# A hybrid decoder block on one core: 80 instead of 256 pair sums in retrieval, all gate masks on VectorE, and the row products behind the last mask

## The chip, the cores and the metric

One core of a Trainium2 chip runs the whole block in one launch. The metric is device time in microseconds (us). The kernel before took 3866.27 us (median of 3 runs, 3858.65 to 3869.51). The engines are TensorE (PE, with its weight loads PEld), VectorE (DVE), ScalarE (ACT), GpSimd (POOL) and SyncE (SP, which only issues transfers here). Each engine works through its own instructions strictly in the order in which they stand.

## The reference

The block is a mixer (windowed attention beside a state space model), a retrieval of single-neuron experts ("PEER"), and a final norm. The change lies in the retrieval, for 512 tokens, 8 heads, 128 keys for each half, the best 16 of each:

```python
def peer(h, w_query, sub_keys, expert_down, expert_up):
    q = (hf @ w_query).reshape(t, PEER_HEADS, 2, PEER_HALF)
    sc = jnp.einsum('thcd,hckd->thck', q, sub_keys)
    s_top, i_top = lax.top_k(sc, PEER_TOPK)                       # 16 of 128, twice
    cand = s_top[:, :, 0, :, None] + s_top[:, :, 1, None, :]      # 16 x 16 sums
    cand_idx = i_top[:, :, 0, :, None] * PEER_NKEYS + i_top[:, :, 1, None, :]
    best, sel = lax.top_k(cand.reshape(t, PEER_HEADS, 256), PEER_TOPK)
    idx = jnp.take_along_axis(cand_idx.reshape(t, PEER_HEADS, 256), sel, axis=-1)
    gates = jax.nn.softmax(best, axis=-1)
    # per token: a = x . expert_down[idx]; w = gelu(a) * gates; out = w @ expert_up[idx]
```

Both lists of 16 are sorted, so the sum of places (a, c) can be among the best 16 only if (a + 1)(c + 1) is at most 16.

## The kernel before

Everything is float32 from outside; the large products are made in three passes of a high and a low part (`whi`, `wlo`: ScalarE casts each weight tile, line 185; VectorE or GpSimd subtracts, line 187). Four stages matter here.

**Retrieval** (lines 907 to 957). For each head TensorE makes queries and scores; VectorE then takes the best 16 of 128 for each half and each of four blocks of 128 tokens (`top16`, lines 847 to 852: maximum of eight, its places, replace, again), adds all 16 x 16 pairs (`cand`, line 932), takes the best 16 of 256, and turns a place into the two indices by shift and mask (lines 944 to 951). An index is looked up by comparison with a ramp (`oh`, line 953, VectorE), a product on GpSimd (line 955) and a sum on VectorE (line 956). GpSimd also makes `wlo` of the query weights.

**Gates** (lines 1065 to 1102). Expert number i1 x 128 + i2; the last 160 of the 512 tokens are not treated densely. For the other 352 a dense gate table g_d is built. Sixteen tokens at a time (22 times, each in two halves, so 44) VectorE makes four masks of 128 x 1024 float16: `o1`, `o2` (lines 1088, 1089), and `g0`, `g1` (lines 1091, 1090); three of four `g1` are made on GpSimd (`ptt`). TensorE multiplies them (line 1098, 16 products for eight tokens), ScalarE copies to `stg` (line 1100), and a transfer stores it in DRAM.

**Row products** (`gathered`, lines 1029 to 1054). For the 160 other tokens 320 steps run beside everything else: each fetches one row of 1 MB by an indirect transfer that GpSimd issues (line 1010) and works it off in one long VectorE instruction (line 1016 for 160 "down" rows, lines 1025 and 1027 for 160 "up" rows). The buffers are two (h3_hi, h3_lo) until the second group of the main loop ends, then three. A step of `gathered` is taken by `paced`: 1.0 a block of 16 tokens in the gates, 1.25 at each of 16 places of a main loop group.

**Main loop** (lines 1155 to 1197). 16 groups: eight *forms* (line 1110: 48 matmuls of 352 columns, lines 201 to 203, then gelu) and 16 *up* products of 24 matmuls (lines 1185 to 1187), so 768 matmuls a group. The forms' results are multiplied by the gate table (line 1165), which a transfer `gt` reads back from g_d (line 1157). The first 21 forms are written ahead of the loop (line 1128) and need no gates.

The order on each engine is made when the program is built, by a scheduler that plays the program through with its own durations; it puts those 21 forms between retrieval and gate work as it sees fit.

Of the kernel before, what the change touches and what calls it, by code (L numbers as in the profile page):

```python
# [1 line left out]

# [4 lines left out]
F32 = mybir.dt.float32  # L7
# [3 lines left out]
U32 = mybir.dt.uint32  # L11
AF = mybir.ActivationFunctionType
OP = mybir.AluOpType
# [5 lines left out]
TT = 4  # L19
# [9 lines left out]
TB = 16  # L29
HB = 8  # L30
# [6 lines left out]
A_BUFS = 5  # L37
LEAD = 2
Z_EARLY = 4
GATHER_PACE = 1.25  # L40
GATE_PACE = 1.0
GATE_SCALE = 32768.0
NEG = -3.0e38
MAGIC = 12582912.0
# [15 lines left out]
def hybrid_block(tc, I, out, dbg=None):  # L60
    nc = tc.nc
# [32 lines left out]
    tt, ts, stt = nc.vector.tensor_tensor, nc.vector.tensor_scalar, nc.vector.scalar_tensor_tensor  # L94
# [235 lines left out]
    ptt = nc.gpsimd.tensor_tensor  # L330
# [130 lines left out]
    for i in range(8):  # L461
        p = head[i]
# [301 lines left out]
    for m in range(KT):  # L764
        p = mm_tile()
# [9 lines left out]
    for m in range(8):  # L775
        p = mm_tile()
# [15 lines left out]
    for m in range(KT):  # L792
        p = mm_tile()
# [32 lines left out]
    for m in range(KT):  # L826
        p = mm_tile()
# [16 lines left out]
    tk = pool("tk", "right", bufs=2)  # L844
    keys = tk.tile([128, 16, 128], F32, name="keys", bufs=1)
    nc.sync.dma_start(keys, I["sub_keys"])
    def top16(vals, idx, x, scratch):
        nc.vector.max(out=vals[:, 0:8], in_=x)
        nc.vector.max_index(out=idx[:, 0:8], in_max=vals[:, 0:8], in_values=x)
        nc.vector.match_replace(out=scratch, in_to_replace=vals[:, 0:8], in_values=x, imm_value=NEG)  # L850
        nc.vector.max(out=vals[:, 8:16], in_=scratch)
        nc.vector.max_index(out=idx[:, 8:16], in_max=vals[:, 8:16], in_values=scratch)
# [64 lines left out]
    for hd in range(8):  # L917
        stop = tk.tile([128, TT, 2, 16], F32, name="stop")
        itop = tk.tile([128, TT, 2, 16], U32, name="itop")
        if hd < 2:  # L920
            query_scores(opening[hd], hd, stop, itop, rstd)
        else:
            o = [mm_tile(), mm_tile(), aux_tile()]
            for qt in range(4):
                query_quarter(o, hd, qt, NB)
            query_scores(o, hd, stop, itop)
        best = tk.tile([128, TT, 16], F32, name="best")
        sel = tk.tile([128, TT, 16], U32, name="sel")
        for b in range(TT):
            cand = tk.tile([128, 256], F32, name="cand")  # L930
            cand2 = tk.tile([128, 256], F32, name="cand2")
            tt(cand.rearrange("p (a c) -> p a c", a=16), stop[:, b, 0, :, None].to_broadcast([128, 16, 16]),  # L932
               stop[:, b, 1, None, :].to_broadcast([128, 16, 16]), op=OP.add)
            top16(best[:, b], sel[:, b], cand, cand2)
        e = tk.tile([128, TT, 16], F32, name="ge")
        s8 = tk.tile([128, 2, TT], F32, name="s8")
        tt(e, best, best[:, :, 0:1].to_broadcast([128, TT, 16]), op=OP.subtract)
        act(e, e, AF.Exp)
        nc.vector.tensor_reduce(s8[:, 0], e, axis=AX.X, op=OP.add)
        nc.vector.reciprocal(s8[:, 1], s8[:, 0])  # L940
        tt(pk[:, :, 2, hd], e, s8[:, 1, :, None].to_broadcast([128, TT, 16]), op=OP.mult)
        itf = tk.tile([128, TT, 2, 16], F32, name="itf")
        nc.vector.tensor_copy(itf, itop)
        for c in range(2):
            ai = tk.tile([128, TT, 16], U32, name="ai")
            if c == 0:
                ts(ai, sel, 4, None, op0=OP.logical_shift_right)
            else:
                ts(ai, sel, 15, None, op0=OP.bitwise_and)
            af = tk.tile([128, TT, 16], F32, name="af")  # L950
            nc.vector.tensor_copy(af, ai)
            oh = tk.tile([128, TT, 16, 16], F32, name="oh")
            tt(oh.rearrange("p a b c -> p (a b) c"), iota[:, None, 0:16].to_broadcast([128, TT * 16, 16]),
               af.rearrange("p a b -> p (a b)")[:, :, None].to_broadcast([128, TT * 16, 16]), op=OP.is_equal)
            nc.gpsimd.tensor_tensor(oh, oh, itf[:, :, c, None, :].to_broadcast([128, TT, 16, 16]), op=OP.mult)
            nc.vector.tensor_reduce(pk[:, :, c, hd], oh, axis=AX.X, op=OP.add)
    close(tk)
# [56 lines left out]
    def gather_down(index, f, g, n):  # L1014
        r = rows_of("down_rows", index[:, n:n + 1])
        stt(r, r, 1.0, hrow, op0=OP.mult, op1=OP.mult, accum_out=f[:, n:n + 1])  # L1016
        if n % 16 == 15:
            w = f[:, n - 15:n + 1]
            act(w, w, AF.Gelu_apprx_tanh)
            tt(w, w, g[:, n - 15:n + 1], op=OP.mult)  # L1020
# [8 lines left out]
    def gathered():  # L1029
        downs = [(pick, fit, gate, n) for n in range(128)] + [(pick_x, fit_x, gate_x, n) for n in range(NX)]  # L1030
        ups = [("own", pick, fit, n) for n in range(128)] + [("x", pick_x, fit_x, n) for n in range(NX)]
        y = None
        for i in range(len(downs) + UP_LAG):
            if i < len(downs):
                if i == 128:
                    wide = slice(ND, NB)
                    token_rows(hrow, *(lambda ks, z=z: z[:, ks, None, wide].bitcast(F32).to_broadcast([128, 4, XQ, NX])
                                       for z in (h2_hi, h2_lo)), (("p k (i t) -> p k i t",), {"i": XQ}))
                gather_down(*downs[i])
                yield  # L1040
            if i >= UP_LAG:
                which, index, f, n = ups[i - UP_LAG]
                if n == 0:
                    y = state["gp"].tile([128, KT, 128], F32, name="yrow")
                gather_up(y, index, f, n)
                if which == "own" and n == 127:
                    gather_finish(y)
                if which == "x" and n == NX - 1:
                    for m in range(KT):
                        p = aux_tile()[:, 0:NX]  # L1050
                        nc.tensor.matmul(p, y[:, m], fold, start=True, stop=True)
                        xm = state["x1"][:, m, ND:NB]
                        stt(xm, p, mod[:, 80 + m:81 + m], xm, op0=OP.mult, op1=OP.add)
                yield

    rest = gathered()
    due = [0.0]

    def paced(pace=GATHER_PACE):
        due[0] += pace  # L1060
        while due[0] >= 1.0:
            next(rest, None)
            due[0] -= 1.0

    for b in range(DT):
        p = aux_tile()
        for c in range(3):
            nc.tensor.transpose(p[:, c * 128:(c + 1) * 128], pk[:, b, c].rearrange("p a b -> p (a b)"), ident)
        ix = gw.tile([128, 4, 128], F16, name="ix")
        gf = gw.tile([128, 128], F32, name="gf")  # L1070
        nc.scalar.copy(ix[:, 0:2].rearrange("p a b -> p (a b)"), p[:, 0:256])
        act(gf, p[:, 256:384], AF.Copy, scale=GATE_SCALE)
        nc.vector.tensor_copy(ix[:, 2], gf)
        tt(ix[:, 3], gf, ix[:, 2], op=OP.subtract)
        for tb in range(128 // TB if b < DT - 1 else (128 - NX) // TB):
            paced(GATE_PACE)
            stg = gw.tile([128, 128, TB], F32, name="stg")
            for hb in range(TB // HB):
                t0_ = tb * TB + hb * HB

                def tok(c):
                    return ix[:, c, t0_:t0_ + HB].rearrange("p (a b) -> p a b", b=2)[:, :, None, :].to_broadcast(shp)

                def one(name):
                    return gw.tile(shp, F16, name=name, tag=name)

                o1, o2, g0, g1 = (one(n_) for n_ in ("o1", "o2", "g0", "g1"))
                tt(o1, iob, tok(0), op=OP.is_equal)
                tt(o2, iob, tok(1), op=OP.is_equal)  # L1089
                (tt if (tb * (TB // HB) + hb) % 4 == 3 else ptt)(g1, o2, tok(3), op=OP.mult)  # L1090
                tt(g0, o2, tok(2), op=OP.mult)
                for q4 in range(HB // 4):
                    p = aux_tile()
                    for q in range(4):
                        a, e = divmod(q4 * 4 + q, 2)
                        o = p[:, q * 128:(q + 1) * 128]
                        for n_, gx in enumerate((g0, g1)):
                            nc.tensor.matmul(o, o1[:, a, :, e], gx[:, a, :, e], start=(n_ == 0), stop=(n_ == 1))
                    c0 = hb * HB + q4 * 4
                    act(stg[:, :, c0:c0 + 4].rearrange("p i t -> p t i"), p.rearrange("p (t i) -> p t i", t=4), AF.Copy,  # L1100
                        scale=1.0 / GATE_SCALE)
            nc.scalar.dma_start(g_d[:, b * (128 // TB) + tb], stg)
# [52 lines left out]
    for g in range(NGRP):  # L1155
# [149 lines left out]
```

## Time and profile before

| what | us |
|---|---|
| median of 3 runs | 3866.27 |
| profiled execution: its time, its span | 3862.01, 3860.2 |
| PE, DVE, ACT, POOL busy in the span | 3572.5, 2757.2, 1295.9, 1006.0 |
| first mask of the gates | 1662.94 |
| first *up* matmul of the main loop | 1920.62 |

The profile is one execution. A row gives us from the span's start, or busy us and the mean ns of one instruction. PE durations overlap each other (a matmul of 352 columns is listed with some 320 ns while the next starts 160 ns later); DVE starts overlap by some 80 ns.

### The profile page before, as it was taken

How to read it: one execution, taken by the hardware profiler on the slowest of the kernel's cores; microseconds unless marked ns; L12 is line 12 of the kernel's file. 1: busy time of each engine (PE TensorE's matmuls, PEld its weight loads, DVE VectorE, ACT ScalarE, POOL GpSimd, SP SyncE). 2: the span in 40 equal slices, each digit the busy share in tenths (PEclk: the TensorE clock that was granted, in tenths of full speed). 3: DMA queues.
4: the chain of work that ended last, by engine and by line, in shares of the span. 5: the costliest groups of instructions: out<-in, count | busy, mean ns of one | idle time of the engine just before them, and what ended most of it. 6: DMA issues, size and time to landing. Idle time of an engine off the chain costs nothing.

```text
span 3860.2 us, 51341 instructions
## 1 busy us (share of the span) xinstructions
PE 3572.5 (93%) x20045; PEld 3242.9 (84%) x20045; DVE 2757.2 (71%) x3948; ACT 1295.9 (34%) x1790; POOL 1006.0 (26%) x851
## 2 busy tenths in 40 slices
PE   7699999999999988887399999999999999998997
PEld 3477777777788888787389999999999999998997
DVE  7644445556863389999887888888867888857844
ACT  3232223334443332345323223333333233333323
POOL 7644520010000245255322212222202122212102
PEclk8889889999999999999599999999999999999999
DMA  8543345447954322267788899999976999958943
GB/s 294 195 154 87 115 147 178 166 161 290 330 168 161 126 64 74 83 245 289 270 324 327 337 336 348 345 343 353 347 251 246 334 342 344 340 179 290 327 128 113
DMA packets 274104, 921.60 MB, mean 239 GB/s; under 512 B 35394, under 2 KB 92866, under 8 KB 229956
## 3 DMA queue, kind: packets, MB, share of 16 engines
q1 hardware_dynamic: 204260, 533.91, 39.8%
q0 software_dynamic: 50048, 344.55, 24.5%
q10 hardware_dynamic: 19552, 39.85, 2.7%
q8 instruction: 157, 2.57, 0.3%
q14 instruction: 87, 0.71, 0.1%
HBM read 871.03 MB, written 47.12 MB: 238 GB/s over the span
## 4 chain that ended last, share of the span: by engine, by line
PE 64%; DVE 13%; issue 10%; DMA 7%; POOL 2%; ACT 1%; DVEq 0%; POOLq 0%; SPq 0%; ACTq 0%
PE mm L203 13%; PE mm L201 13%; PE mm L202 13%; PE aux L1187 6%; PE aux L1186 6%; PE aux L1185 6%; DVE wlo L187 2%; DMA rows<-in_up_rows,pick 1%; DMA rows<-in_down_rows,pick 1%; DMA gt<-g_d 1%; DMA raw<-in_up 1%; DVE rows L1016 1%; POOL rows L1010 1%; DVE cand L932 1%; DVE o L1089 1%
## 5 line engine op out<-in xcount | busy, mean ns | idle before, releaser
L185 ACT CAST whi<-raw 128x1024 fp32r<-128x1024 f32 (+2 forms) x744 | 759.3, 1022 | 1736.1 <-PE mm L202 811.2
L187 DVE TENSOR_TENSOR wlo<-raw,whi 128x1024 fp32r<-128x1024 f32 (+2 forms) x696 | 868.2, 1248 | 435.4 <-ACT whi L185 403.8
L203 PE MATMUL mm<-h_hi,wlo 128*128 128x352 f32 (+1 forms) x2752 | 955.5, 347 | 41.8 <-DVE wlo L187 41.6
L201 PE MATMUL mm<-h_hi,whi 128*128 128x352 f32 (+1 forms) x2752 | 952.2, 346 | 8.1 <-ACT whi L185 8.1
L202 PE MATMUL mm<-h_lo,whi 128*128 128x352 f32 (+1 forms) x2752 | 949.1, 345 | 0.0
L1185 PE MATMUL aux<-wh,whi 128*128 128x352 f32 x2048 | 667.7, 326 | 39.4 <-ACT wh L191 22.4
L1187 PE MATMUL aux<-wh,wlo 128*128 128x352 f32 x2048 | 669.8, 328 | 27.2 <-DVE wlo L187 27.1
L1186 PE MATMUL aux<-wl,whi 128*128 128x352 f32 x2048 | 667.9, 326 | 2.3 <-DVE wl L192 2.3
L203 PEld LDWEIGHTS mm<-h_hi,wlo 128*128 128x128 f32 x2752 | 525.9, 191 | 79.8 <-DVE wlo L187 50.1
L201 PEld LDWEIGHTS mm<-h_hi,whi 128*128 128x128 f32 x2752 | 525.7, 191 | 40.6 <-ACT whi L185 9.7
L202 PEld LDWEIGHTS mm<-h_lo,whi 128*128 128x128 f32 x2752 | 527.1, 192 | 32.0 <-issue 4.4
L1185 PEld LDWEIGHTS aux<-wh,whi 128*128 128x128 f32 x2048 | 390.7, 191 | 45.9 <-ACT whi L185 23.3
L1187 PEld LDWEIGHTS aux<-wh,wlo 128*128 128x128 f32 x2048 | 390.4, 191 | 35.1 <-DVE wlo L187 34.7
L1186 PEld LDWEIGHTS aux<-wl,whi 128*128 128x128 f32 x2048 | 390.3, 191 | 3.4 <-DVE wl L192 3.4
L1016 DVE SCALAR_TENSOR_TENSOR rows<-rows,hrow 128x2048 f32<-128x2048 f32 x160 | 370.3, 2316 | 18.8 <-DMA rows<-in_down_rows,pick 18.2
L140 DVE SCALAR_TENSOR_TENSOR adaw<-adaw,cb 128x1024 f32<-128x1024 f32 x176 | 227.3, 1298 | 146.5 <-DMA adaw<-in_w_ada 146.4
L1010 POOL DMA_INDIRECT rows<-in_up_rows,pick x128 | 151.7, 1185 | 577.2 <-DVE rows L1016 479.3
L1027 DVE SCALAR_TENSOR_TENSOR yrow<-rows,fit,yrow 128x2048 f32<-128x2048 f32 x127 | 297.8, 2345 | 4.1 <-DMA rows<-in_up_rows,pick 4.1
L1010 POOL DMA_INDIRECT rows<-in_down_rows,pick x128 | 151.8, 1186 | 525.4 <-DVE yrow L1027 291.6
L1188 DVE SCALAR_TENSOR_TENSOR x<-aux,mod,x 128x352 f32<-128x352 f32 x256 | 148.6, 581 | 181.2 <-PE aux L1187 180.8
L213 POOL TENSOR_TENSOR rstd<-rstd,t 128x512 f32<-128x512 f32 (+2 forms) x42 | 50.7, 1207 | 661.7 <-ACT t L211 661.0
L187 POOL TENSOR_TENSOR wlo<-raw,whi 128x1024 fp32r<-128x1024 f32 (+1 forms) x48 | 105.9, 2211 | 115.4 <-ACT whi L185 114.0
(431 smaller groups left out, 4696.1 us busy)
## 6 DMA issues: line engine op xcount, KB each, us to landing
raw<-in_down SPq DMA_DIRECT2D x256, 512.0 KB
raw<-in_up SPq DMA_DIRECT2D x256, 512.0 KB
adaw<-in_w_ada SPq DMA_DIRECT2D x192, 512.0 KB
raw<-in_w_in SPq DMA_DIRECT2D x88, 512.0 KB
g_d<-stg ACTq DMA_DIRECT2D x22, 1024.0 KB
gt<-g_d SPq DMA_DIRECT2D x16, 1408.0 KB
raw<-in_w_out SPq DMA_DIRECT2D x32, 512.0 KB
raw<-in_w_query SPq DMA_DIRECT2D x32, 512.0 KB
```

Of the source, the lines that this page charges most:

```text
L140: stt(w, w, 1.0, cb[:, half], op0=OP.mult, op1=OP.mult, accum_out=part[:, half:half + 1])
L185: nc.scalar.copy(h, r)
L187: sub(l, r, h.bitcast(F32), op=OP.subtract)
L201: nc.tensor.matmul(p, h[:, k], (xh[kk] if isinstance(xh, list) else xh[:, kk]), start=first, stop=False)
L202: nc.tensor.matmul(p, h[:, k], (xl[kk] if isinstance(xl, list) else xl[:, kk]), start=False, stop=False)
L203: nc.tensor.matmul(p, l[:, k], (xh[kk] if isinstance(xh, list) else xh[:, kk]), start=False, stop=last)
L1010: nc.gpsimd.indirect_dma_start(out=r.rearrange("p k c -> p (k c)"), out_offset=None, in_=I[table], in_offset=bass.IndirectOffsetOnAxis(ap= ...
L1016: stt(r, r, 1.0, hrow, op0=OP.mult, op1=OP.mult, accum_out=f[:, n:n + 1])
L1027: stt(y, r, f[:, n:n + 1], y, op0=OP.mult, op1=OP.add)
L1185: nc.tensor.matmul(p, h[:, j], WH[j], start=(j == 0), stop=False)
L1186: nc.tensor.matmul(p, h[:, j], WL[j], start=False, stop=False)
L1187: nc.tensor.matmul(p, l[:, j], WH[j], start=False, stop=(j == GI - 1))
```

## The change

First, `cand` has 80 places: 16 for (0, c), then 7 x 8 for a of 1 to 7 and c of 0 to 7, then 8 for (8 to 15, 0). Six additions a head stand for four, `top16` runs over 80 elements, and nine small operations turn a place into two indices. Second, all four masks are made on VectorE. Third, the gates take no steps of `gathered` any more, its first two row products are ordered behind the last mask on VectorE (the order holds on that engine only; their transfers are not held), and its pace in the main loop is 1.35.

```diff
-GATHER_PACE = 1.25
-GATE_PACE = 1.0
+GATHER_PACE = 1.35
...
+        cand = tk.tile([128, TT, 80], F32, name="cand")
+        s1, s2 = stop[:, :, 0], stop[:, :, 1]
+        tt(cand[:, :, 0:16], s2, s1[:, :, 0:1].to_broadcast([128, TT, 16]), op=OP.add)
+        tt(cand[:, :, 72:80], s1[:, :, 8:16], s2[:, :, 0:1].to_broadcast([128, TT, 8]), op=OP.add)
         for b in range(TT):
-            cand = tk.tile([128, 256], F32, name="cand")
-            cand2 = tk.tile([128, 256], F32, name="cand2")
-            tt(cand.rearrange("p (a c) -> p a c", a=16), stop[:, b, 0, :, None].to_broadcast([128, 16, 16]),
-               stop[:, b, 1, None, :].to_broadcast([128, 16, 16]), op=OP.add)
-            top16(best[:, b], sel[:, b], cand, cand2)
+            tt(cand[:, b, 16:72].rearrange("p (a c) -> p a c", a=7), s1[:, b, 1:8, None].to_broadcast([128, 7, 8]),
+               s2[:, b, None, 0:8].to_broadcast([128, 7, 8]), op=OP.add)
+        for b in range(TT):
+            cand2 = tk.tile([128, 80], F32, name="cand2")
+            top16(best[:, b], sel[:, b], cand[:, b], cand2)
...
-        for c in range(2):
-            ai = tk.tile([128, TT, 16], U32, name="ai")
-            if c == 0:
-                ts(ai, sel, 4, None, op0=OP.logical_shift_right)
-            else:
-                ts(ai, sel, 15, None, op0=OP.bitwise_and)
-            af = tk.tile([128, TT, 16], F32, name="af")
-            nc.vector.tensor_copy(af, ai)
+        nc.vector.tensor_copy(place, sel)
+        ts(ai, sel, 3, None, op0=OP.logical_shift_right)
+        nc.vector.tensor_copy(af, ai)
+        ts(af, af, -1.0, 0.0, op0=OP.add, op1=OP.max)
+        stt(af, place, -64.0, af, op0=OP.add, op1=OP.max)
+        stt(bf, place, -64.0, af, op0=OP.add, op1=OP.subtract)
+        stt(sf, af, 1.0, af, op0=OP.min, op1=OP.add)
+        stt(sf, sf, -8.0, place, op0=OP.mult, op1=OP.add)
+        tt(bf, bf, sf, op=OP.max)
+        for c, at_ in enumerate((af, bf)):
...
-                gather_down(*downs[i])
+                with tc.issue_after(masked) if i < len(slots) else contextlib.nullcontext():
+                    gather_down(*downs[i])
...
         for tb in range(128 // TB if b < DT - 1 else (128 - NX) // TB):
-            paced(GATE_PACE)
...
-                (tt if (tb * (TB // HB) + hb) % 4 == 3 else ptt)(g1, o2, tok(3), op=OP.mult)
                 tt(g0, o2, tok(2), op=OP.mult)
+                masked = tt(g1, o2, tok(3), op=OP.mult).ins
```

Lines behind the change stand 1 to 13 further down: line 187 is 188 now, 1016 is 1028, 1088 to 1091 are 1101 to 1104, 1185 is 1198.

On VectorE, in the decoding of a late head of the retrieval (`sel` the 16 places, `af` and `bf` the two indices, `oh` the comparison with the ramp that GpSimd then multiplies), before:

```order
L947 TENSOR_SCALAR ai<-sel 128x64
L949 TENSOR_SCALAR ai<-sel 128x64
L851 MAX stop<-scores_10990 128x8
L939 TENSOR_REDUCE s_10760<-ge 128x4
L852 MAX_INDEX itop<-stop,scores_10984 128x8
L951 CAST af<-ai 128x64 x2
L852 MAX_INDEX itop<-stop,scores_10990 128x8
L940 RECIPROCAL s_10760<-s_10760 128x4
L850 MATCH_REPLACE scores_11006<-stop,scores 128x128
L953 TENSOR_TENSOR oh<-iota,af 128x1024 x2
```

and after:

```order
L958 SCALAR_TENSOR_TENSOR af<-place,af 128x64
L948 TENSOR_TENSOR pk<-ge,s_10774 128x4x16
L959 SCALAR_TENSOR_TENSOR bf<-place,af 128x64
L960 SCALAR_TENSOR_TENSOR sf<-af 128x64
L965 TENSOR_TENSOR oh<-iota,af 128x1024
L961 SCALAR_TENSOR_TENSOR sf<-sf,place 128x64
L962 TENSOR_TENSOR bf<-bf,sf 128x64
L965 TENSOR_TENSOR oh<-iota,bf 128x1024
L968 TENSOR_REDUCE pk<-oh 128x4x16
```

The two comparisons stood side by side; now two operations of two tensors stand between them, right behind the first comparison, which sets GpSimd going.

On VectorE late in the gates (o: masks of lines 1088 and 1089, g: of 1091 and 1090; rows: a row product), before:

```order
L1091 TENSOR_TENSOR g_13080<-o_13079,ix 128x1024
L1016 SCALAR_TENSOR_TENSOR rows,fit<-rows,hrow 128x2048
L1091 TENSOR_TENSOR g_13108<-o_13107,ix 128x1024
L1089 TENSOR_TENSOR o_13140<-iota_12044,ix 128x1024
L1088 TENSOR_TENSOR o_13139<-iota_12044,ix 128x1024
L1091 TENSOR_TENSOR g_13141<-o_13140,ix 128x1024
L1089 TENSOR_TENSOR o_13168<-iota_12044,ix 128x1024
L1016 SCALAR_TENSOR_TENSOR rows,fit<-rows,hrow 128x2048
```

and the end of the gates after:

```order
L188 TENSOR_TENSOR wlo<-raw,whi 128x1024
L1102 TENSOR_TENSOR o_13384<-iota_12084,ix 128x1024
L1103 TENSOR_TENSOR g_13357<-o_13356,ix 128x1024
L1101 TENSOR_TENSOR o_13355<-iota_12084,ix 128x1024
L1104 TENSOR_TENSOR g_13358<-o_13356,ix 128x1024
L1103 TENSOR_TENSOR g_13385<-o_13384,ix 128x1024
L1101 TENSOR_TENSOR o_13383<-iota_12084,ix 128x1024
L1104 TENSOR_TENSOR g_13386<-o_13384,ix 128x1024
L1028 SCALAR_TENSOR_TENSOR rows,fit<-rows,hrow 128x2048 x2
L188 TENSOR_TENSOR wlo<-raw,whi 128x1024 x2
L1028 SCALAR_TENSOR_TENSOR rows,fit<-rows,hrow 128x2048 x2
L1178 TENSOR_TENSOR a_13414<-a_13414,gt 128x352
```

Before, 24 row products stand ahead of the last mask; after, none does, and four stand between it and the first product with the gate table.

On TensorE at the end of the gates (mm: a form, aux<-g: masks, aux<-wh: the first *up* product), before:

```order
L1098 LDWEIGHTS o_13411
L1098 MATMUL aux<-g_13413,o_13411 128x128
L1098 LDWEIGHTS o_13411
L1098 MATMUL aux<-g_13414,o_13411 128x128
L1185 MATMUL aux<-wh,whi 128x352 x2
```

and after:

```order
L1111 LDWEIGHTS o_13383
L1111 MATMUL aux<-g_13358,o_13355 128x128
L1111 LDWEIGHTS o_13383
L1111 MATMUL aux<-g_13386,o_13383 128x128
L202 MATMUL mm<-h_hi,whi 128x352
L203 MATMUL mm<-h_lo,whi 128x352
L204 MATMUL mm<-h_hi,wlo 128x352
L1198 MATMUL aux<-wh,whi 128x352 x2
```

Before, the last 272 of the 704 mask matmuls stand without a form's matmul among them; after, forms stand between the mask matmuls to the end. Ahead of the first transposes of the gates stand 360 matmuls of forms before, and 242 after; of 1008 in all.

Row steps on VectorE, counted by main loop group (to the group's last addition to the output): before, 24 ahead of the loop, then 15, 14, 23, 24, 24, 24, 24, 24, 5, 28, 24, 24, 11, 19, 13, 0; after, none ahead of it, then 15, 15, 18, 24, 24, 24, 24, 24, 24, 25, 24, 24, 23, 19, 13, 0.

## Rows read from the trace of the kernel before

**Rows 1.** Busy time by stretch: us, PE, PEld, DVE, ACT, POOL, clock, DMA share, GB/s.

```profile
1350.00:1660.00 310.00, 262.44 (x1577) 255.68 (x1577) 294.35 (x989) 96.20 (x161) 130.16 (x56) 0.94 0.24 75
1660.00:1900.00 240.00, 172.68 (x1357) 161.69 (x1355) 234.35 (x231) 118.08 (x137) 125.30 (x65) 0.82 0.74 272
...
2361.00:2862.00 501.00, 495.31 (x3071) 493.51 (x3070) 418.79 (x396) 161.59 (x195) 101.54 (x92) 1.00 0.93 341
2862.00:2994.00 132.00, 127.61 (x793) 126.37 (x793) 86.83 (x89) 42.61 (x53) 22.10 (x13) 1.00 0.66 233
```

**Rows 2.** What PE waited for, 1350 to 1925: us, times, longest.

```profile
PE aux L1098 <- DVE g L1091: 29.8, 10, 6.4
PE mm L203 <- DVE wlo L187: 29.4, 14, 4.7
```

**Rows 3.** VectorE by line, 1350 to 1660: busy us, mean ns, idle before.

```profile
L932 DVE TENSOR_TENSOR cand<-stop 128x256 f32<-128x256 f32 x32 | 38.5, 1203 | 0.0
...
L941 DVE TENSOR_TENSOR pk<-ge,s 128x64 f32<-128x64 f32 x8 | 15.7, 1964 | 0.0
L848 DVE MAX8 stop<-scores 128x8 f32<-128x128 f32 x64 | 14.4, 272 | 0.0
...
L848 DVE MAX8 best<-cand 128x8 f32<-128x256 f32 x32 | 13.1, 408 | 0.0
...
L951 DVE CAST af<-ai 128x64 f32<-128x64 uint32 x16 | 2.2, 175 | 0.0
...
L937 DVE TENSOR_TENSOR ge<-best 128x64 f32<-128x64 f32 x8 | 1.6, 200 | 0.0
```

**Rows 4.** Line 932, all 32: ns min/median/max, first and last start.

```profile
L932 DVE TENSOR_TENSOR cand<-stop x32: 396/770/2655, 1409.9 to 1636.1; 128x256 f32<-128x256 f32 x32
```

**Rows 5.** GpSimd by line, 1350 to 1660.

```profile
L187 POOL TENSOR_TENSOR wlo<-raw,whi 128x1024 fp32r<-128x1024 f32 x28 | 72.0, 2577 | 82.7 <-ACT whi L185 81.3 <-issue 1.3
L955 POOL TENSOR_TENSOR oh<-oh,itf 128x1024 f32<-128x1024 f32 x16 | 44.6, 2802 | 97.3 <-DVE oh L953 97.3
```

**Rows 6.** VectorE by line, 1660 to 1925.

```profile
L1016 DVE SCALAR_TENSOR_TENSOR rows<-rows,hrow 128x2048 f32<-128x2048 f32 x28 | 68.9, 2462 | 6.1 <-DMA rows<-in_down_rows,pick 6.1
L187 DVE TENSOR_TENSOR wlo<-raw,whi 128x1024 fp32r<-128x1024 f32 x28 | 48.5, 1732 | 2.1 <-ACT whi L185 2.1
L1089 DVE TENSOR_TENSOR o<-iota,ix 128x1024 f16<-128x1024 f16 x44 | 44.7, 1025 | 1.8 <-POOL g L1090 1.8
```

**Rows 7.** VectorE in order of time, start and end of the gates: start, us.

```profile
1662.94 0.69 DVE L1088 TENSOR_TENSOR o<-iota,ix 128x1024 f16<-128x1024 f16 x1 [1.43 <-ACT ix L1071]
...
1861.04 0.68 DVE L1090 TENSOR_TENSOR g<-o,ix 128x1024 f16<-128x1024 f16 x1
1861.64 0.68 DVE L1089 TENSOR_TENSOR o<-iota,ix 128x1024 f16<-128x1024 f16 x1
...
1862.84 2.38 DVE L1089 TENSOR_TENSOR o<-iota,ix 128x1024 f16<-128x1024 f16 x1
...
1895.71 0.68 DVE L1090 TENSOR_TENSOR g<-o,ix 128x1024 f16<-128x1024 f16 x1
...
1906.96 2.29 DVE L1016 SCALAR_TENSOR_TENSOR rows<-rows,hrow 128x2048 f32<-128x2048 f32 x1 [5.03 <-DMA rows<-in_down_rows,pick]
```

**Rows 8.** TensorE in order of time, inside the gates and at the first *up* product.

```profile
1686.63 2.01 PE L1098 MATMUL aux<-g,o 128*128 128x128 f16 x32
1688.44 0.41 PE L203 MATMUL mm<-h_hi,wlo 128*128 128x352 f32 x1
...
1920.62 0.95 PE L1185 MATMUL aux<-wh,whi 128*128 128x352 f32 x2 [22.40 <-ACT wh L191]
```

**Rows 9.** SyncE in order of time, loads of the gate table, one a group.

```profile
2092.34 0.53 SPq L1157 DMA_DIRECT2D gt<-g_d  x1
2231.76 0.59 SPq L1157 DMA_DIRECT2D gt<-g_d  x1
```

**Rows 10.** VectorE by line, 2361 to 2862: the weight subtraction.

```profile
L187 DVE TENSOR_TENSOR wlo<-raw,whi 128x1024 fp32r<-128x1024 f32 x128 | 156.3, 1221 | 57.6 <-ACT whi L185 57.1
```

More of the change, by code (lines that the diff above doesn't have):

```diff
@@ L1 @@
+import contextlib
 import numpy as np
@@ L943, in hybrid_block @@
         nc.vector.tensor_copy(itf, itop)
-        for c in range(2):
-            ai = tk.tile([128, TT, 16], U32, name="ai")
-            if c == 0:
-                ts(ai, sel, 4, None, op0=OP.logical_shift_right)
-            else:
-                ts(ai, sel, 15, None, op0=OP.bitwise_and)
-            af = tk.tile([128, TT, 16], F32, name="af")
-            nc.vector.tensor_copy(af, ai)
+        ai = tk.tile([128, TT, 16], U32, name="ai")
+        place, af, bf, sf = (tk.tile([128, TT, 16], F32, name=n_) for n_ in ("place", "af", "bf", "sf"))
+        nc.vector.tensor_copy(place, sel)
[8 more added lines that the diff above has]
+        for c, at_ in enumerate((af, bf)):
             oh = tk.tile([128, TT, 16, 16], F32, name="oh")
             tt(oh.rearrange("p a b c -> p (a b) c"), iota[:, None, 0:16].to_broadcast([128, TT * 16, 16]),
-               af.rearrange("p a b -> p (a b)")[:, :, None].to_broadcast([128, TT * 16, 16]), op=OP.is_equal)
+               at_.rearrange("p a b -> p (a b)")[:, :, None].to_broadcast([128, TT * 16, 16]), op=OP.is_equal)
             nc.gpsimd.tensor_tensor(oh, oh, itf[:, :, c, None, :].to_broadcast([128, TT, 16, 16]), op=OP.mult)
@@ L1057, in hybrid_block, with paced @@
     due = [0.0]
-    def paced(pace=GATHER_PACE):
-        due[0] += pace
+    def paced():
+        due[0] += GATHER_PACE
         while due[0] >= 1.0:
```

## The prediction

> **What bounds the kernel now.** I read busy time by stretch first. It shows two kernels in one. In the four main loop groups from 2361 to 2862 TensorE is busy 495.3 of 501 us: 125.25 us a group, 0.163 us for each of 768 matmuls. Ahead of the loop it is VectorE: 294 of 310 us in retrieval and 234 of 240 in the gates, while TensorE is busy 262 and 173 and its clock falls from 0.94 to 0.82 of full speed on average [rows 1]. The list of TensorE's waits names what it lacks there: masks from VectorE (29.8 us for `g` alone) and weight halves from VectorE (29.4) [rows 2]. So a microsecond of VectorE work taken out between 1350 and 1896 shortens the run, until TensorE's own work there is the longer; one added in the main loop costs nothing as long as TensorE stays fed.
>
> The lines of VectorE then tell what it does there. Two kinds of time are in them: work, and being held up by GpSimd. A pair sum takes 0.396 us free, 1.203 in the mean and up to 2.655 [rows 3, 4]; a mask 0.60 us from start to start, but 2.38 when GpSimd is at its own mask [rows 7]. Reading instructions of one tensor (maxima, casts) show no such spread.
>
> **Retrieval, part by part.** VectorE is never free here, so the sum goes one to one.
>
> Pair sums: 32 took 38.5 us, of which 32 x 0.396 = 12.7 is work and 25.8 blocked [rows 3, 4]. Now 48 small ones at no more than the 0.200 of a 64 element operation of two tensors [rows 3]: 9.6. Saved: 3.1 of work.
>
> `top16`: one maximum takes 408 ns over 256 and 272 over 128 elements, 1.06 ns an element; 176 fewer elements save 0.187 us. With five instructions of that kind in 32 blocks: 160 x 0.187 = 29.9 us.
>
> Decoding: four operations a head go (32 x 0.175 = 5.6), nine come; four at 0.175 and five of two tensors at 0.200, 1.7 us a head, 13.6 in all [rows 3]. Added: 8.0. Work together: -25.0.
>
> Blocked time: now 25.8 in pair sums and 8 x (1.964 - 0.200) = 14.1 in line 941, 39.9 together [rows 3]. GpSimd's work there, 72.0 + 44.6 = 116.6 us, stays [rows 5]. The new order puts `sf` right behind the comparison that sets off a GpSimd product of 2.80 us, so it waits for nearly all of that in each head: some 2.3 us, 18.4 in all. The other 28 GpSimd instructions may catch a two-tensor operation as often as now, 25.8. Together 44.2, so +4.3. The ends are no blocking at all (-39.9) and every GpSimd instruction blocking in full (+76.7); I take the middle one, since it comes from the same neighbours. What bears on it in the Trainium skill ("SBUF — State Buffer", section "Who interferes with whom") is that a VectorE operation with two SBUF tensors and a GpSimd instruction that reads SBUF share a pair of ports, which the first to start holds for its whole instruction. The rows agree as to who is hit (0.396 against 2.655); by the rule alone, fifteen such operations a head instead of eight are so many more targets, and it is the rule that would bring the upper end, a rival below.
>
> The order also places 118 fewer form matmuls ahead of the gates, 2.5 forms with two subtractions of 1.22 us each [rows 10]: 6.0 us moved behind. First mask: 1662.9 [rows 7] - 25.0 + 4.3 - 6.0 = 1636.
>
> **Gates.** From the first mask to the end of the last were 233 us [rows 7]. What goes from VectorE: 24 row products ahead of the last mask at 2.46 us (59), and the blocking: 1.025 us a mask of line 1089 and 1.732 us a subtraction stand against 0.60 and 1.22 free [rows 6, 7, 10]. What comes: 33 masks from GpSimd, 0.60 each (20). What stays is 176 x 0.60 + 29 x 1.22 = 106 + 35 = 141 us. GpSimd has nothing left there but two row transfers ahead of the masks, so I take the free durations; if a second source of blocking were there, the present means would give 176 x 1.0 + 29 x 1.73 = 226, the upper bound.
>
> But now TensorE is later. Behind the first transposes stand 1008 - 242 = 766 form matmuls, 125 us at 0.163, and 704 mask matmuls at (1688.44 - 1686.63)/32 = 0.057 us [rows 8], 40 us: 165. Before, it had 648 form matmuls there, was done with them long before the last mask, and came to the masks' pace, its clock at 0.82 in the mean [rows 1]; forms now stand among the masks to the end. So the stage takes 165 us by TensorE, 141 by VectorE, and I add 8 for the two waiting for each other in turn (between 0 and 35, a quarter of VectorE's work): last mask matmul at 1636 + 173 = 1809.
>
> **From the gates to the loop.** The last block must be stored, read back and multiplied; TensorE stood 22.4 us for that [rows 8], and the forms are used up here too. It stays. Four row products stand ahead of the first product with the gate table. The transfers of the first two were issued long ago, the next two follow as the buffers come free. Before, three stood there, the last waiting 5.03 us for its transfer and done at 1909.3, ten us ahead of need [rows 7, 8]; a fourth, two us or so later, still fits. First *up* matmul: 1831 against 1920.6, 90 us sooner.
>
> **Main loop.** The 24 rows land here, 24 x 2.3 us of VectorE and 24 MB. By the count of steps they do not lengthen it: they fill groups 8 and 12, which had 5 and 11, and the stream still ends in group 14. Groups of 24 rows run at 125.25 us with TensorE 99% busy; the group from 2862, without rows for most of its length, took 132 [rows 1]. I take 0, between -12 (no gaps and restarts any more) and +74 (24 rows x 1.05 MB at the 341 GB/s of the full groups [rows 1], if transfers bound everywhere).
>
> **Sum.** 3862 (the profiled execution's own time, 4 below the median) - 90 = 3772; on the median's scale 3776.
>
> **Rivals.**
> - *The two engines do not mesh in the gates.* Form matmuls wait for a subtraction that stands behind masks, masks wait for buffers that TensorE frees. At 200 us instead of 173 the run ends 27 later: 3803. For it: `wlo` was TensorE's second wait [rows 2]. Against: VectorE has 24 us to spare.
> - *The rows are paid back in the loop.* All 24 at the transfer rate: +74, 3850. For it: 0.93 DMA share in full groups. Against: those same groups hold TensorE at 99% [rows 1].
> - *Blocking grows to all of GpSimd's work in retrieval* : +72 over my sum, 3848. For it: the two-tensor operations nearly double. Against: now the blocking is a third of GpSimd's work. It is what the rule of the Trainium skill's "SBUF — State Buffer" page gives at its fullest.
> - *More is gained:* no blocking on VectorE in retrieval (-44) and a loop without the gap (-8), partly caught by TensorE: 3730.
> - *Slower:* the row stream has lost its slack. From group 3 to 11 there are nine groups of 24 rows in a row, 217 steps, and each waits in VectorE's order in front of subtractions that TensorE needs. The group from 2092 to 2231 took 139.4 us with 23 rows, 6.1 us a row [rows 9], against 5.2 in full groups. If the longer chain ran at 6.1, it would cost 217 x 0.84 = 182 us: 3958. It ends above before from 0.41 us a row. Against: five full groups in succession already ran at 5.2.
>
> **Chances.** Forecast 0.58 (its own range 3755 to 3795), not meshing 0.17, rows paid back 0.08, blocking 0.03, more gained 0.10, slower 0.04. The range 3735 to 3825 takes in the forecast, the first rival and half of the larger gain, 0.8. About 12 us, 0.3%, is what a measurement can tell: faster in all but the slower case and a part of the two paid-back ones: 0.94; same 0.02; slower 0.04.
>
> **What would show it.** In the changed profile: `top16` over 80 at some 0.22 us; `sf` behind the first comparison at over 2 us; masks all at 0.68 listed; TensorE over 90% busy in the gates and its clock there above 0.9; first mask near 1636, first *up* matmul near 1831; then 125 us a group through groups 3 to 11, without the gap after 2840. I am wrong if the first *up* matmul is later than 1860, or the loop from it to the end takes over 1955 us (before: 1939.6, from 1920.62 to 3860.2).

## The result, and the profile after

The changed kernel took 3754.59 us (median of 4 runs, 3739.47 to 3761.78) against 3867.89 (4 runs, 3858.65 to 3871.11): ratio 0.971, 95% interval 0.9688 to 0.9732. That is 113 us sooner; 90 were forecast, 3776 with a range of 3735 to 3825. Run again among the experiments it took 3746.85 (ratio 0.9691, 0.967 to 0.9713). The profiled execution, 3761.78 us with a span of 3760.0, is the slowest of the first four, so its own 100 us are the smaller figure; another execution of the same kernel (e0_after, below) lies 13 us lower.

First the stretches of the changed kernel (us, PE, PEld, DVE, ACT, POOL, clock, DMA share, GB/s), which answer to [rows 1]:

```profile
1350.00:1623.00 273.00, 240.54 (x1478) 234.17 (x1477) 255.41 (x1042) 89.30 (x154) 126.29 (x61) 0.95 0.24 80
1623.00:1787.00 164.00, 163.27 (x1446) 156.60 (x1444) 147.20 (x217) 119.74 (x136) 2.42 (x2) 1.00 0.65 241
1787.00:1813.00 26.00, 0.00 (x0) 0.00 (x0) 7.82 (x9) 2.84 (x5) 3.58 (x4) 0.59 0.95 341
...
2245.00:2758.00 513.00, 501.15 (x3071) 498.12 (x3070) 427.00 (x403) 161.39 (x195) 107.99 (x96) 0.99 0.92 338
2758.00:2890.00 132.00, 128.47 (x788) 127.78 (x787) 110.73 (x106) 42.19 (x53) 27.22 (x25) 0.97 0.91 336
```

The bound has changed sides in the gates: TensorE is busy 163.27 of 164 us at full clock, VectorE 147 and GpSimd hardly at all. Before, VectorE was busy 234 of 240 and the clock 0.82. In TensorE's list of waits from 1350 to 1790 no mask is left; the first lines of it, which answer to [rows 2], belong to retrieval:

```profile
PE mm L866 <- POOL wlo L188: 15.0, 7, 6.0
PE mm L864 <- ACT whi L186: 6.5, 2, 3.7
PE mm L204 <- DVE wlo L188: 5.2, 4, 2.1
```

The places that bound the stages, VectorE and then TensorE in order of time (start, us), answer to [rows 7, 8]:

```profile
1623.44 0.68 DVE L1101 TENSOR_TENSOR o<-iota,ix 128x1024 f16<-128x1024 f16 x1
...
1781.77 0.68 DVE L1104 TENSOR_TENSOR g<-o,ix 128x1024 f16<-128x1024 f16 x1
1782.37 2.28 DVE L1028 SCALAR_TENSOR_TENSOR rows<-rows,hrow 128x2048 f32<-128x2048 f32 x1
...
1800.14 2.29 DVE L1028 SCALAR_TENSOR_TENSOR rows<-rows,hrow 128x2048 f32<-128x2048 f32 x1 [4.53 <-DMA rows<-in_down_rows,pick]
...
1812.02 3.57 DVE L1178 TENSOR_TENSOR a<-a,gt 128x352 f32<-128x352 f32 x8 [9.58 <-DMA gt<-g_d]
```

```profile
1813.15 0.95 PE L1198 MATMUL aux<-wh,whi 128*128 128x352 f32 x2 [26.88 <-ACT wh L192]
```

| us, profiled executions | before | after | difference | forecast |
|---|---|---|---|---|
| first mask | 1662.9 | 1623.4 | -39.5 | -27 |
| first mask to start of last mask matmul | 235.0 | 162.1 | -72.9 | -62 |
| from there to the first *up* matmul | 22.7 | 27.7 | +5.0 | 0 |
| from there to the end | 1939.6 | 1946.8 | +7.2 | 0 |

Retrieval by line of VectorE (busy us, mean ns, idle before), which answers to [rows 3]:

```profile
L962 DVE TENSOR_TENSOR bf<-bf,sf 128x64 f32<-128x64 f32 x8 | 12.0, 1498 | 0.1
L965 DVE TENSOR_TENSOR oh<-iota,bf 128x1024 f32<-128x1024 f32 x8 | 11.8, 1476 | 0.2
L937 DVE TENSOR_TENSOR cand<-stop 128x56 f32<-128x56 f32 x32 | 11.2, 351 | 0.0
L961 DVE SCALAR_TENSOR_TENSOR sf<-sf,place 128x64 f32<-128x64 f32 x8 | 10.9, 1362 | 0.0
...
L849 DVE MAX8 best<-cand 128x8 f32<-128x80 f32 x32 | 5.3, 223 | 0.0
...
L935 DVE TENSOR_TENSOR cand<-stop 128x32 f32<-128x32 f32 x8 | 5.0, 627 | 0.0
...
L934 DVE TENSOR_TENSOR cand<-stop 128x64 f32<-128x64 f32 x8 | 4.3, 544 | 0.0
...
L960 DVE SCALAR_TENSOR_TENSOR sf<-af 128x64 f32<-128x64 f32 x8 | 1.7, 216 | 0.0
...
L948 DVE TENSOR_TENSOR pk<-ge,s 128x64 f32<-128x64 f32 x8 | 1.7, 215 | 0.0
```

A maximum over 80 takes 223 ns (some 220 forecast). The pair sums fell from 38.5 to 11.2 + 5.0 + 4.3 = 20.5 us. `sf` and `bf` stand at 1.36 and 1.50 where the same kind of operation takes 0.216 next to them, so they carry 19.4 us of waiting for GpSimd; line 948, the old line 941, has lost its own (1.964 to 0.215, 14.0 us).

In the gates the masks and the subtraction are at their free durations, which answers to [rows 6]:

```profile
L188 DVE TENSOR_TENSOR wlo<-raw,whi 128x1024 fp32r<-128x1024 f32 x31 | 37.9, 1221 | 11.5 <-ACT whi L186 9.1 <-ACT stg L1113 2.0
L1101 DVE TENSOR_TENSOR o<-iota,ix 128x1024 f16<-128x1024 f16 x44 | 30.1, 684 | 6.6 <-ACT ix L1085 6.6
```

### The profile page after: what moved, and what is told of

It is laid out like the page before. It is cut to its first block, busy times and chain, and to the rows that moved or that the text cites. A ratio compares the mean times of both kernels' runs of the same rounds, so it can differ in the third digit from the quotient of the medians.

```text
span 3760.0 us, 51345 instructions
## 1 busy us (share of the span) xinstructions
PE 3551.0 (94%) x20045; PEld 3227.8 (86%) x20045; DVE 2686.4 (71%) x4037; ACT 1291.9 (34%) x1788; POOL 906.7 (24%) x818
## 4 chain that ended last, share of the span: by engine, by line
PE 76%; DVE 8%; DMA 7%; issue 2%; ACT 1%; POOL 1%; SPq 0%; DVEq 0%; ACTq 0%; POOLq 0%
PE mm L204 15%; PE mm L202 15%; PE mm L203 15%; PE aux L1200 8%; PE aux L1199 8%; PE aux L1198 8%; DMA gt<-g_d 3%; DMA raw<-in_up 2%; DVE wlo L188 1%; PE aux L1111 1%; DMA iraw<-km_d 1%; PE aux L664 1%; ACT whi L186 1%; PE aux L700 1%; PE aux L727 1%
## 5 line engine op out<-in xcount | busy, mean ns | idle before, releaser
L188 DVE TENSOR_TENSOR wlo<-raw,whi 128x1024 fp32r<-128x1024 f32 (+2 forms) x696 | 851.6, 1224 | 424.9 <-ACT whi L186 400.8
L1200 PE MATMUL aux<-wh,wlo 128*128 128x352 f32 x2048 | 673.6, 330 | 25.5 <-DVE wlo L188 25.4
L204 PEld LDWEIGHTS mm<-h_hi,wlo 128*128 128x128 f32 x2752 | 523.6, 190 | 44.0 <-DVE wlo L188 14.2
```

The costliest lines, as they stand in the source:

```text
L188: sub(l, r, h.bitcast(F32), op=OP.subtract)
L204: nc.tensor.matmul(p, l[:, k], (xh[kk] if isinstance(xh, list) else xh[:, kk]), start=False, stop=last)
L1200: nc.tensor.matmul(p, l[:, j], WH[j], start=False, stop=(j == GI - 1))
```

## The experiments

Each was timed against the kernel before on the same chip; the ratio has its 95% interval. A stage's time is that of the one profiled execution: the gates go from the first mask to the start of the last mask matmul, the wait from there to the first *up* matmul, the loop from there to the end. The name behind a heading is the one by which later text points at the run.

**One part alone: the pair sums (e1_pairs).** The kernel before with the whole first part of the change, `cand` and decoding, and nothing else of it.

```diff
-            cand = tk.tile([128, 256], F32, name="cand")
+        cand = tk.tile([128, TT, 80], F32, name="cand")
...
```

> Only the 80 pair sums and their decoding; gates, masks and row products as before. My theory (VectorE bounds retrieval, so its savings there count one to one): the changed kernel's first mask stood 39.5 us sooner, of which some 6 was form work moved behind it, so -33 here: about 3834 us, gates as long as before (235 us from the first mask to the last mask matmul). Rival (TensorE or GpSimd catches up, the gates take it back): not below 3857.

3824.49 us, ratio 0.9883 (0.9848 to 0.9917): -43 in the medians. The first mask stood at 1626.5, 36.4 sooner, but the gates took 242.6 from there (235.0 before): the forms that no longer stand ahead of them bring five more weight subtractions into them (32 against 27), and VectorE still bounds them there. The first *up* matmul came 28.6 sooner, the loop was 7.4 shorter. So the saving in retrieval came through, less what moved into the gates; the theory holds there, not in that the gates stay as long, and the loop's part of the -43 is not explained by it.

**The masks alone (e2_masks).** The kernel before with this edit:

```diff
-                (tt if (tb * (TB // HB) + hb) % 4 == 3 else ptt)(g1, o2, tok(3), op=OP.mult)
                 tt(g0, o2, tok(2), op=OP.mult)
+                masked = tt(g1, o2, tok(3), op=OP.mult).ins
```

> Only the masks: all four on VectorE, row products still in the gates (the order now puts 35 of them ahead of the last mask, 24 before). My theory (the masks alone free VectorE of blocking, but the rows fill it again): 176 x 0.60 + 28 x 1.22 + 35 x 2.3 = 220 us of VectorE against 233, so -13, about 3854, and up to -30 with the 11 rows that are done early. Rival (blocking by GpSimd was the whole loss): -70, about 3797.

3846.51 us, ratio 0.994 (0.9919 to 0.9961): -21. The blocking is gone, and rows have taken its room. Its stretch of the gates, then VectorE's lines in it:

```profile
1654.00:1880.00 226.00, 168.62 (x1338) 154.97 (x1337) 219.18 (x285) 116.96 (x136) 49.28 (x42) 0.84 0.92 336
```

```profile
L1016 DVE SCALAR_TENSOR_TENSOR rows<-rows,hrow 128x2048 f32<-128x2048 f32 x37 | 84.5, 2283 | 6.4 <-DMA rows<-in_down_rows,pick 6.4
...
L1088 DVE TENSOR_TENSOR o<-iota,ix 128x1024 f16<-128x1024 f16 x44 | 29.9, 682 | 0.5 <-issue 0.5
```

VectorE is still busy 219 of 226 us, 84.5 of them in 37 row products that the scheduler drew into the time set free. The rival (-70) is out.

**The rows alone (e3_rows).** The kernel before with the third part; `masked` is here the last g0, which stands last there.

```diff
-GATHER_PACE = 1.25
+GATHER_PACE = 1.35
...
-                gather_down(*downs[i])
+                with tc.issue_after(masked) if i < len(slots) else contextlib.nullcontext():
+                    gather_down(*downs[i])
...
-            paced(GATE_PACE)
```

> Only the rows: none in the gates, first two behind the last mask, pace 1.35; three of four g1 masks still on GpSimd. My theory (row products are work of VectorE that goes one to one): -59 in the gates, +7 in the main loop, about 3815; masks still show 2.38 us when GpSimd is at work. Rival (the rows only hid behind GpSimd's blocking): not below 3850.

3815.2 us, ratio 0.9865 (0.9837 to 0.9894): -52, as expected in the sum; the gates gave 51.6 of the 59 expected and the loop cost 3.2 of the 7. GpSimd's masks are the limit that is left there (e4_gates takes them away as well); `o2` (line 1091 here, 1089 before) waits for them and is held up by them:

```profile
L1091 DVE TENSOR_TENSOR o<-iota,ix 128x1024 f16<-128x1024 f16 x44 | 52.8, 1217 | 16.1 <-POOL g L1092 16.1
```

**Masks and rows together (e4_gates).** The changed kernel with the whole first part taken back.

```diff
-        cand = tk.tile([128, TT, 80], F32, name="cand")
+            cand = tk.tile([128, 256], F32, name="cand")
...
```

> Masks and rows together, pair sums as before. My theory: VectorE 176 x 0.60 + 28 x 1.22 = 140 us, TensorE 577 x 0.163 + 40 = 134, so some 150 from first mask to last mask matmul against 235; with +5 in the gap and +7 in the loop -73, about 3794; and together with e1_pairs the whole change (-113) within 12. Rival (TensorE-bound as in the whole change): 163 us there, about 3807.

3769.32 us, ratio 0.9762 (0.9725 to 0.98): -98, more than either theory gave, and more than -21 and -52 together. From first mask to last mask matmul it took 154.8 us (150 expected):

```profile
1662.00:1817.00 155.00, 149.70 (x1338) 141.76 (x1337) 140.09 (x210) 115.90 (x134) 1.83 (x4) 0.98 0.68 248
```

Both engines are near their work here, 150 and 140 us. Each half of the change takes away only one of VectorE's two burdens; the masks' half gave little because rows filled the room. Of the -98, or -98.7 in the profiled execution, 84.5 stand ahead of the first *up* matmul; the loop gave 14.2, where +7 was expected.

With e1_pairs it makes -141, 28 more than the whole change. Stage by stage the parts do add up where they work:

| us against before, profiled executions | first mask | gates | wait | loop | all |
|---|---|---|---|---|---|
| e1_pairs | -36.4 | +7.6 | +0.2 | -7.4 | -36.0 |
| e4_gates | -0.6 | -80.2 | -3.7 | -14.2 | -98.7 |
| both added | -37.0 | -72.6 | -3.5 | -21.6 | -134.7 |
| the whole change | -39.5 | -72.9 | +5.0 | +7.2 | -100.2 |
| the whole change again (e0_after) | -42.1 | -73.0 | +1.5 | +0.2 | -113.4 |

The gates are longer in the whole than in e4_gates because forms that no longer fit beside the shorter retrieval (314 instead of 431 form matmuls stand ahead of the first mask matmul) come into them; but that price, 7.6 us, is in e1_pairs already. The missing 28 us lie behind the last mask matmul, most of them in the loop, and why the loop was shorter in the two parts is not shown.

**The changed kernel again (e0_after), and three variants of it, timed together.**

> The changed kernel once more, as the measure for the three beside it. Its own four runs lay between 3739 and 3762. My theory of that spread: it lies in the main loop (the same rows a group took 1947 us in the changed kernel's profile and 1925 in e4_gates), so another profile shows the same 162 us in the gates and another loop. Rival: the spread lies ahead of the loop.

3746.85 us (3736.82 to 3753.09). In its profile the gates took 162.0 us, the wait 24.2, the loop 1939.8; in the first profile 162.1, 27.7 and 1946.8; e4_gates, with the same rows a group, had 19.0 and 1925.4. So of the 13 us between the two executions 7.0 are in the loop, 3.5 in the wait and 2.6 ahead of the first mask, in the main as the theory says; what moves it from execution to execution was not found, nor whether the 1925.4 of e4_gates is such a spread or belongs to that kernel.

Both comparisons behind the decoding (e5_decode):

```diff
-        tt(bf, bf, sf, op=OP.max)
+        decoded = tt(bf, bf, sf, op=OP.max).ins
...
-            tt(oh.rearrange("p a b c -> p (a b) c"), iota[:, None, 0:16].to_broadcast([128, TT * 16, 16]),
+            with tc.issue_after(decoded):
+                tt(oh.rearrange("p a b c -> p (a b) c"), iota[:, None, 0:16].to_broadcast([128, TT * 16, 16]),
...
```

> The changed kernel, but both comparisons of a head stand behind the whole decoding, side by side again. In the changed kernel sf takes 1.36 us and bf 1.50 in the mean, 0.2 free: 19.7 us of blocking by GpSimd. My theory: it goes, the first mask comes 12 to 18 us sooner, the whole 10 to 16 faster than e0_after. Rival (GpSimd's lock only finds the next operation of two tensors, or VectorE waits for the product itself): 0.

3762.06 us, ratio 0.9729 (0.9707 to 0.975): 15 more than e0_after. My theory fell, and the rival was too mild. `sf` and `bf` came to 0.218 us each, but the waiting went on to the next operation of two tensors, the second comparison (1.48 us before the edit, 2.50 now), and then to the sum, which now waits for the product itself (2.4 us of idle time before the edit):

```profile
L966 DVE TENSOR_TENSOR oh<-iota,bf 128x1024 f32<-128x1024 f32 x8 | 20.0, 2495 | 0.0
L969 DVE TENSOR_REDUCE pk<-oh 128x64 f32<-128x1024 f32 x14 | 16.9, 1204 | 8.8 <-POOL oh L968 8.8
```

So nothing was gained: ahead of the first mask VectorE was busy 252.5 us, 2.6 less than in e0_after. That the first mask stood at 1634.8 instead of 1620.8 is idle time of VectorE: 6.4 us more of it for the product, and 7.7 us in one wait for ScalarE that e0_after does not have there. The edit also moved other work in the order (79 more matmuls ahead of the first mask), so the 15 us are not the price of the blocking alone.

The rows spread evenly (e6_even):

```diff
         while due[0] >= 1.0:
-            next(rest, None)
+            with tc.issue_after(added[-1]) if added else contextlib.nullcontext():
+                next(rest, None)
...
-            stt(x1[:, m, 0:ND], p, mod[:, 80 + m:81 + m], x1[:, m, 0:ND], op0=OP.mult, op1=OP.add)
+            added.append(stt(x1[:, m, 0:ND], p, mod[:, 80 + m:81 + m], x1[:, m, 0:ND], op0=OP.mult, op1=OP.add).ins)
```

> The changed kernel, with every row step ordered on VectorE behind the last addition to the output written before it: 21 to 25 rows a group instead of 24 in each and then a gap. My theory (the rows do not bound the loop): same as e0_after within 5 us. Rival (groups of 24 rows lack transfers for TensorE's weights, an even stream does not): 10 to 15 faster.

3828.38 us, ratio 0.9905 (0.9883 to 0.9926): 82 slower than e0_after, which neither expected. 79 of them are in the loop, 2018.9 us from the first *up* matmul, where TensorE's waits are now led by:

```profile
PE aux L1202 <- DVE wlo L188: 35.3, 35, 5.3
PE mm L204 <- DVE wlo L188: 30.6, 20, 3.7
```

(In the changed kernel the same two have 25.4 and 4.5 us.) The order it forces delays TensorE's weights on VectorE; these waits are 36 of the 79 us, and the rest was not followed further. It says nothing of transfers.

Two forms held back for the wait (e8_gap):

```diff
     for i2 in range(EARLY * GI + A_BUFS):
-        form(i2)
+        with tc.issue_after(gated) if i2 >= EARLY * GI + A_BUFS - 2 else contextlib.nullcontext():
+            form(i2)
```

(`gated` is the last mask matmul.)

> The changed kernel, with the last 2 of the 21 early forms (96 matmuls, 15.7 us) ordered behind the last mask matmul on TensorE. My theory (TensorE bounds the gates now, 162 us, VectorE needs 147): gates about 149, and the two forms run in the wait for the gate table, so 10 to 14 faster than e0_after. Rival (the gates are held by both engines taking turns, not by TensorE's work): 0 to 4 faster.

3735.18 us, ratio 0.9669 (0.9651 to 0.9688): 12 below e0_after in the medians, though the intervals overlap. The stages go the theory's way, in the gates by less than half of it: they took 156.4 us instead of 162.0, where about 149 was expected, the first *up* matmul stood at 1797.0 instead of 1807.0, and TensorE was busy in the wait:

```profile
1621.00:1777.00 156.00, 150.13 (x1341) 142.91 (x1340) 140.45 (x211) 114.58 (x131) 1.63 (x4) 0.98 0.67 246
1777.00:1797.00 20.00, 16.71 (x107) 16.12 (x104) 12.93 (x14) 7.90 (x11) 7.12 (x4) 0.98 0.92 325
```

**Three forms held back (e9_gap3).** The 2 in the edit above is 3.

> The changed kernel with 3 instead of 2 early forms (144 matmuls, 23.5 us) behind the last mask matmul. My theory: e8_gap left TensorE 4 us idle in the wait and 6 in the gates; VectorE's 141 us there are now close: 0 to 4 faster than e8_gap, about 3733. Rival (forms still running when the gate table arrives hold the first up products back): 4 to 8 slower than e8_gap.

3730.86 us, ratio 0.964 (0.9615 to 0.9665): the fastest kernel that computes the whole block, below the changed kernel in median and interval, though by little in the interval; against e8_gap it can't be told apart. In its profile the first *up* matmul stands at 1809.0 all the same, 12 us later than in e8_gap and 2 later than in e0_after. It is not what the rival feared: the third form ended at 1801, and TensorE then stood until the weights of the first *up* product had come in (the cast of them on ScalarE, then the matmul):

```profile
1807.88 1.04 ACT L186 CAST whi<-raw 128x1024 fp32r<-128x1024 f32 x1 [6.41 <-DMA raw<-in_up]
```

```profile
1809.02 0.63 PE L1199 MATMUL aux<-wh,whi 128*128 128x352 f32 x1 [8.05 <-issue]
```

What the median gained stands in the loop, 1920.1 us against 1939.8 in e0_after, and no run here shows why.

**The index product on VectorE (e10_oh).**

```diff
-            nc.gpsimd.tensor_tensor(oh, oh, itf[:, :, c, None, :].to_broadcast([128, TT, 16, 16]), op=OP.mult)
+            tt(oh, oh, itf[:, :, c, None, :].to_broadcast([128, TT, 16, 16]), op=OP.mult)
```

> The changed kernel, with the product oh x itf of the index lookup on VectorE instead of GpSimd (16 products of 128 x 1024). My theory (in retrieval the GpSimd product costs VectorE as much in blocking, some 22 us in sf, bf and oh, as it would cost as work, 16 x 1.2 = 19): same as e0_after within 6 us, sf and bf back at 0.2. Rival (the chain comparison, product, sum over two engines also delays the head's end): 10 to 20 faster.

3746.08 us, ratio 0.9699 (0.9675 to 0.9723): no change, as the theory says. But `sf` and `bf` did not come back to 0.2:

```profile
L967 DVE TENSOR_TENSOR oh<-oh,itf 128x1024 f32<-128x1024 f32 x16 | 22.7, 1416 | 0.0
...
L961 DVE SCALAR_TENSOR_TENSOR sf<-sf,place 128x64 f32<-128x64 f32 x8 | 5.3, 668 | 0.0
...
L962 DVE TENSOR_TENSOR bf<-bf,sf 128x64 f32<-128x64 f32 x8 | 4.8, 600 | 0.0
```

The 22.7 us of work stand for 12.8 us less in `sf` and `bf`; GpSimd's subtractions hold up what the products leave alone (an `sf` that started at 1505.70 took 1.90 us, with a subtraction on GpSimd from 1504.11 to 1507.51).

**Both of these together (e11_both),** edits as above.

> e9_gap3 and e10_oh together. My theory: effects add, as one lies in retrieval and the other behind it: about 3730. Rival: GpSimd's relief in retrieval only moves waiting into the gates, where TensorE is the bound: as e9_gap3.

3736.05 us, ratio 0.9655 (0.9634 to 0.9677): not to be told from e9_gap3. Since e10_oh by itself changed nothing, this does not decide between theory and rival; the first mask stood at 1639.8 there, 19 later than in e9_gap3, which was not followed.

**The price of the rows in the loop (e7_eighth).** 280 of the 320 row products and transfers are left out, the steps stay, so the result is not the block's.

```diff
+        if n % 8 == 0:
             r = rows_of("down_rows", index[:, n:n + 1])
...
+        if n % 8:
+            return
         r = rows_of("up_rows", index[:, n:n + 1])
```

> The changed kernel with only every eighth row fetched and multiplied, 40 of 320; the steps stay at their places (280 row products and their transfers are left out). My theory (the rows hardly bound the main loop): the loop from the first up matmul takes 1900 to 1915 us against 1940 to 1947, so a row costs some 0.1 us and the 24 moved ones 3. Rival (a row costs what its transfer takes, 3.1 us): if even a third of the rows were so paid, the loop would lose 290 us.

3693.06 us, the loop 1877.8 us; I had said 1900 to 1915. Most of its groups follow each other in 123.53 us, by the loads of the gate table:

```profile
2228.90 0.53 SPq L1175 DMA_DIRECT2D gt<-g_d  x1
...
2352.43 0.53 SPq L1175 DMA_DIRECT2D gt<-g_d  x1
...
2475.97 0.53 SPq L1175 DMA_DIRECT2D gt<-g_d  x1
```

Against the loops of e4_gates and the changed kernel (1925 to 1947) the 280 rows cost 48 to 69 us, 0.17 to 0.25 us a row. That is the price of transfer and product together. For 24 rows it is 4 to 6 us, not the 74 of the paid-back rival.

## Why the prediction was right

**The sum.** 3754.59 was measured, 3776 forecast, at the lower edge of the forecast's own range of 3755 to 3795. The two stages up to the last mask matmul were sized too carefully, by 12.5 and 10.9 us, the two behind it too hopefully, by 5.0 and 7.2 in that execution, so a part of the errors cancelled.

**VectorE bounds retrieval and the gates: shown.** With work taken from VectorE in one of the two stages alone, the first *up* matmul came 28.6 us sooner (e1_pairs) and 52.0 (e3_rows), against 33 and 59 expected ahead of the loop.

**`top16`: right.** At 223 ns over 80 elements against 408 the step is the one predicted; its five instructions gave 32.3 us, 29.9 forecast.

**Blocking in retrieval: mis-sized, on the careful side.** The forecast had `sf` right in place and near in size, and it missed that `bf` behind it would wait as well: 19.4 us for both, 18.4 forecast for `sf` alone. Its sum priced eight products and the 28 subtractions of GpSimd and left out the other eight products. What failed most is "may catch a two-tensor operation as often as now, 25.8". The least times of the new pair sums (ns min/median/max) show what is work in their 20.5 us:

```profile
L934 DVE TENSOR_TENSOR cand<-stop x8: 198/202/1710, 1412.4 to 1598.5; 128x64 f32<-128x64 f32 x8
L935 DVE TENSOR_TENSOR cand<-stop x8: 160/168/2141, 1405.6 to 1594.4; 128x32 f32<-128x32 f32 x8
L937 DVE TENSOR_TENSOR cand<-stop x32: 187/192/2109, 1402.4 to 1587.2; 128x56 f32<-128x56 f32 x32
```

That is 8.8 of work and 11.7 of blocking. With 2.2 in the second comparison and 2.2 in a cast (below) the blocking is some 35.5 us: 4.4 less than before, where 4.3 more was forecast. These 9 us are most of the 12.5 by which the first mask came sooner than forecast. That the blocking goes on to the next operation when its victim is taken away e5_decode shows; and with the products taken away (e10_oh) GpSimd's subtractions still block.

The Trainium skill's page ("SBUF — State Buffer", section "Who interferes with whom") was drawn on only for two tensors. It also counts casts and copies in a two-port mode among those that can contend, and the trace agrees: one `itf` cast of eight (line 950), 0.200 us at the least, took 2.404, from just behind the start of a GpSimd subtraction to just behind its end. My sentence that casts show no spread held for the trace of before and not for this one:

```profile
1456.64 2.37 POOL L188 TENSOR_TENSOR wlo<-raw,whi 128x1024 fp32r<-128x1024 f32 x1
1456.70 2.40 DVE L950 CAST itf<-itop 128x128 f32<-128x128 uint32 x1
L950 DVE CAST itf<-itop x8: 200/216/2404, 1413.1 to 1598.6; 128x128 f32<-128x128 uint32 x8
```

**TensorE takes over in the gates: right, and the 8 us for taking turns were not needed.** 165 us of matmuls were forecast, 162.1 measured without a mask wait. The not-meshing rival is out. e8_gap shows the bound from the other side, in part: 15.7 us of form work taken out made the stage 5.6 us shorter, with TensorE busy 150 and VectorE 140 of 156. So close to VectorE's work the two do wait for each other.

**The wait stays: right within its spread.** 27.7 and 24.2 us in two profiles, 19.0 in e4_gates. As forecast, the fourth row product was done (1802.4) well ahead of the gate table (1812).

**The rows fit into the loop: right in size; a sign named for it did not come.** By e7_eighth they cost about 5 us. The slower rival would have needed 0.41 us for each of 217 rows; the whole price is 0.25 at most. The sign was 125 us a group in groups 3 to 11 and no gap after 2840. The loads of the gate table follow each other here in 129.1 us in the mean (128.0 in e0_after, 127.5 before for the same groups):

```profile
2114.23 0.53 SPq L1170 DMA_DIRECT2D gt<-g_d  x1
...
2758.41 0.53 SPq L1170 DMA_DIRECT2D gt<-g_d  x1
2890.07 0.53 SPq L1170 DMA_DIRECT2D gt<-g_d  x1
...
3276.19 0.53 SPq L1170 DMA_DIRECT2D gt<-g_d  x1
```

The stretch that took 132 us before, with 14 row products in it, takes 132 again (2758 to 2890) with 26, so it was not the missing rows that made it long. Four full groups took 513 us in the first profile where before had 501, with the same 24 rows in each; e0_after had 511. So the +7 of the loop there is no more than the spread between executions and kernels (1925 to 1947 us with the rows of a group unchanged, 1940 and 1947 for the same kernel), and whether the price of the rows is in it stays open.

## What to carry to other kernels

Before summing the savings of several edits on a bounding engine, look up how much work the next engine has in that stage, and what the scheduler will draw into the room: here one half alone gave 21 us because row products filled it, and with both halves TensorE was busy 163 of the 164 us. Add parts up stage by stage: by their whole times they missed the whole by 28 us, in the stages that they touch by some 5. When a VectorE operation waits for GpSimd, moving it can hand the wait to the next one, as in e5_decode; price the GpSimd instruction, not the victim. And once an engine bounds a stage that ends in a round trip through DRAM, keep some of its work that needs nothing from that trip for the wait, as much as fits: two forms brought the first *up* matmul forward by 10 us, with three it stood where it was.

## What the hardware showed that was not expected

A cast of one tensor can wait for GpSimd as well, 2.404 us against 0.200. And the 1.05 MB row transfers, at 0.92 busy share of the transfer engines, cost the loop only 0.17 to 0.25 us each, VectorE's product included, where one takes 3.1 us at the 338 GB/s of the full groups (an estimate): most of that time ran beside TensorE's work.
